# A seventh gate block ahead of the z blocks, 14 of its runs behind the last u, w products, and scan steps with 3 + 3 runs of projections

## The chip, the cores and the metric

The kernel runs on one core of a Trainium2 chip. The metric is the device time of one execution in microseconds; several executions are timed and their median is given. The engines are named as in the profile: PE (matrix products), PEld (its weight loads), DVE (vector), ACT (scalar and activation functions), POOL and SP (here used for issuing transfers). Each engine works through its own queue in order, and a transfer is issued by an engine's queue and lands some time later.

## The reference

One layer of a hybrid decoder block on x of 1 x 1024 x 1024, in float32. Two token mixers run on the same normalised input, each result is multiplied by its own SiLU gate path (z), projected up, weighted by per-channel sigmoid gates, summed and projected out; a residual add and a final RMSNorm follow. Mixer A is attention with three dilated windows. Mixer B, where the change acts, is a gated delta rule, computed in chunks of 64 tokens:

```python
def _gated_delta_rule(q, k, v, g, beta):
    ...
    t_inv = lax.linalg.triangular_solve(eye + a, jnp.broadcast_to(eye, a.shape),
                                        left_side=True, lower=True, unit_diagonal=True)
    u = t_inv @ (vc * bc[..., None])
    w = t_inv @ (k_beta * jnp.exp(G)[..., None])
    attn = jnp.einsum('bhnid,bhnjd->bhnij', qc, kc) * decay_incl
    ...
    def step(state, inp):
        q_e, at, u_c, w_c, k_d, dec = inp
        v_new = u_c - jnp.einsum('bhck,bhkv->bhcv', w_c, state)
        o = jnp.einsum('bhck,bhkv->bhcv', q_e, state) + jnp.einsum('bhij,bhjv->bhiv', at, v_new)
        state = state * dec[..., None, None] + jnp.einsum('bhck,bhcv->bhkv', k_d, v_new)
        return state, o
```

There are 8 heads and 16 chunks, so the scan has 16 steps, one after another.

## The kernel before

The large work of PE is the projections of the normalised input (h, held as a high and a low half in fp16) with the input weights (whi and wlo). The **feed** cuts these into units, one per block of 256 weight columns, and each unit into runs. A run is one `feed.tick(1)`: three products of 128x512 at L183, L184 and L185. Most units have 32 runs; some, among them gates 0, 6 and 7 and the four z blocks, are computed with seven products in place of eight (28 runs) and give their four outputs after runs 16, 20, 24 and 28. The feed takes the units in the order in which they were added. A unit's weights are loaded (L313, on POOL's queue) and split into halves (ACT at L330, DVE at L329 and L83) while the unit ahead of it still runs.

PE's order is written out by hand: everything on PE stands in program order. Wherever mixer B has to wait for another engine, the code calls `feed.tick(n)`, and n runs of projections stand between the two products that depend on each other. How many stand where is set by the constants at L44 to L72. The other engines are ordered by a scheduler by data and priorities.

The stages around the change, in program order:

- **Merge** (twice, for the head halves hb = 0 and 1): the triangular inverses are put together from 32x32 blocks (L1350, L1365). `MERGE_TICKS` runs stand in two gaps of each. Y is the intermediate result that DVE copies.
- **u, w products** (L1413, L1417), in two groups g for each hb. `UW_LAG[1][hb]` runs stand ahead of the first group and `UW_LAG[2]` behind each group but the last. Their results are copied to uw tiles (L1424, by DVE for u and by ACT for w) that share three buffers, and stored to un_d (POOL's queue, L1429) and wn_d (ACT's queue, L1426).
- **Pairs** (L1266): the score products of the chunks, in banks ps_S and ps_G. Right ahead of hb = 1's stand `Q_LAG[1]` = 4 runs. E, their masked result, is stored to a_d (POOL's queue, L1630). Sums and transposed products on ps_O (L1247) follow.
- `feed.until(("gate", 5))`, then the pools are changed; from there on gate outputs use a tile gst with two buffers in place of one.
- **Scan** (L1706, L1723, L1734): each step multiplies the state Sb with w and q (ps_S, L1706), DVE forms vn, PE multiplies vn with the decayed keys (ps_G, L1723), and DVE adds to Sb (L86 is the helper's line for these DVE operations). `PACE[0]` runs stand between L1706 and L1723, `PACE[1]` behind L1723. Each second step ends with the products of vn and the score matrix (L1734) into ob. `SCAN_LEAD` runs stand ahead of the first step.
- **Turn loops** (L1755): after `OB_LAG` runs, ob times the factor fac of its norm is transposed in four loops; two head pairs h0 by two halves hf. Each takes a bank of ps_G and one of ps_S, of which there are two each, and DVE multiplies them into zb, four writes a loop. Four runs stand behind each loop.

A gate output is a tanh of the product into gst (L948) and a store to gspa or gspb (L950); for two of a seven-product unit's four outputs DVE first combines product and rest into gst. A z output of mixer A (zs) is a SiLU, a product with mixer A's result (oa, loaded on SP's queue) and a split into osa; of mixer B a SiLU into zb. `UW_LAG` and the other constants are module constants; `state_side` calls the merge and the u, w products.

Of the kernel before, what the change touches and what calls it, by code (L numbers as in the profile page):

```python
# [51 lines left out]
K_LAG = 4  # L52
Q_LAG = (14, 4)
Q_SUMS = (8, 3)
PACE = (4, 3)
UW_LAG = (12, (10, 4), 6)
STATE_LAG = 12
OB_LAG = 12
ZS = 1
# [1 line left out]
OG = 2  # L61
TURN_LAG = 20
SUMS_AT = (4, 36, 68, 100)
MERGE_TICKS = 5
V_GAP = 8
GM_LAG = 2
BA_LAG = 8
# [10 lines left out]
def hybrid_block(ctx: ExitStack, tc: tile.TileContext, A):  # L78
# [13 lines left out]
    def bank(tag, bufs):  # L92
        return ps.tile([128, 512], F32, name=f"ps_{tag}", tag=tag, bufs=bufs)
# [99 lines left out]
    def proj(w, ct, hf, out):  # L193

        hi, lo = w
        p = bank("mm", 3)
        cs, ts = slice(ct * 128, ct * 128 + 128), slice(hf * 512, hf * 512 + 512)
        n = 0
        for _ in mm3_steps(p, (lambda k: hi[:, k, cs], lambda k: lo[:, k, cs]),
                           (lambda k: h_hi[:, k, ts], lambda k: h_lo[:, k, ts])):  # L200
            n += 1
            if n == KT:
                out(p)
            yield
# [150 lines left out]
    def seven_products(blocks, out, product=by_channel):  # L355

        x, q = bank("mm", 3), bank("mm", 3)

        def step(n, p, fn, first=False):
            for i, _ in enumerate(product(n, blocks[n], p, first)):  # L360
                if i == 3:
                    fn()
                yield

        def copy(dst, src):
            with tc.high_priority():
                SC.copy(dst, src)

        y, rest = [], []

        def seed_y():
            y.append(bank("mm", 3))
            copy(y[0], x)

        def keep():
            rest.append(wst.tile([128, 512], F32, name="x7", tag="x7", bufs=1))
            copy(rest[0], q)

        yield from step(0, x, seed_y, True)
        yield from step(1, q, keep, True)  # L380
        yield from step(2, x, lambda: copy(q, x))
        yield from step(3, y[0], lambda: out(0, 0, y[0], None))
        yield from step(4, q, lambda: out(1, 1, q, rest[0]))
        yield from step(5, x, lambda: out(1, 0, x, rest[0]))
        yield from step(6, q, lambda: out(0, 1, q, None))

    feed = Feed()

    def add_unit(name, unit, gen, gen7):
        if unit in SEVENS:  # L390
            feed.add(name, Seven(unit), gen7)
        else:
            feed.add(name, Normal(A["w"][unit]), gen)
# [526 lines left out]
    def gate_unit(i, out):  # L920
        br, u = ("a", i) if i < 4 else ("b", i - 4)

        def gen7(w):
            def take(c, hf, p, rest):
                with tc.high_priority():
                    out(br, 2 * u + c, hf, p, rest)

            yield from seven_products(w, take)

        def gen(w):  # L930
            for c in range(2):
                for hf in range(2):
                    def take(p):
                        with tc.high_priority():
                            out(br, 2 * u + c, hf, p)

                    yield from proj(w, c, hf, take)

        add_unit(("gate", i), U_GATE + i, gen, gen7)
# [399 lines left out]
    def merge(hb, T1p, bsp):  # L1339
# [4 lines left out]
        def left(g):  # L1344
            py = bank("S", 2)
            Y = p2_.tile([128, 16, 32], F32, name="Y", tag="rv", bufs=3)
            for n in range(16):
                for c2 in range(2):
                    r = 64 * c2
                    PE.matmul(py[r + 32:r + 64, n * 32:n * 32 + 32], lhsT=flat[r:r + 32, 16 * g + n, 32:64],  # L1350
                              rhs=T1p[r:r + 32, 4 * g + n // 4, n % 4], start=(n == 0), stop=True,
                              skip_group_check=True)
                    yield
            for c2 in range(2):
                r = slice(64 * c2 + 32, 64 * c2 + 64)
                with tc.high_priority():
                    TT(Y[r], py[r].rearrange("p (n i) -> p n i", i=32), bc(bsp[r, 16 * g:16 * g + 16], 32), ALU.mult)
            Ys[g] = Y

        def right(g):  # L1360
            pu, Y = bank("G", 2), Ys[g]
            for n in range(16):
                for c2 in range(2):
                    r = 64 * c2
                    PE.matmul(pu[r:r + 32, n * 32:n * 32 + 32], lhsT=Y[r + 32:r + 64, n],  # L1365
                              rhs=flat[r + 32:r + 64, 16 * g + n, 32:64], start=(n == 0), stop=True,
                              skip_group_check=True)
                    yield
            for c2 in range(2):
                r = slice(64 * c2, 64 * c2 + 32)  # L1370
                with tc.high_priority():
                    SC.copy(flat[r, 16 * g:16 * g + 16, 32:64], pu[r].rearrange("p (n i) -> p n i", i=32))

        Ys = {}
        for _ in left(0):
            pass
        feed.tick(MERGE_TICKS)
        for _ in zip_longest(left(1), right(0)):
            pass
        feed.tick(MERGE_TICKS)  # L1380
        for _ in right(1):
            pass

    def state_parts(hb):

        def load(g):
            ts = slice(4 * g, 4 * g + 4)
            rv = p2_.tile([128, 4, 4, 64], F32, name="rvt", tag="vT", bufs=2)

            tag = ("As", "X")[g] if hb else "vT"  # L1390
            kb = p2_.tile([128, 4, 4, 64], F32, name="kbt", tag=tag, bufs=1 if hb else 2)
            nc.sync.dma_start(out=rv, in_=rv_d[ts, :, 4 * hb:4 * hb + 4].rearrange("t p h v -> p t h v"))
            nc.sync.dma_start(out=kb, in_=kb_d[hb][:, ts])
            return rv, kb
# [3 lines left out]
        for g in range(2):  # L1398
            if g and not hb:
                loads.append(load(g))  # L1400
                feed.tick(UW_LAG[0])
            rv, kb = loads[g]
# [53 lines left out]
    for hb in range(2):  # L1456
        conv_unit(hb, 0, lambda c, hb=hb: qT[2 * hb + c],
                  lambda c, q, hb=hb: nc.scalar.dma_start(out=q_d[2 * hb + c], in_=q))
    gate_unit(5, gate_spill)
    side, solved, packs = [], [], []  # L1460
    for hb in range(2):
        decay(hb)
# [11 lines left out]
    def z_unit(br, u, take):  # L1474
        def gen(w):
            def out(c, hf, p, rest):
                with tc.high_priority():
                    take(br, 2 * u + c, hf, p, rest)

            yield from seven_products(w, out)  # L1480

        feed.add(("z", br, u), Seven(U_Z + 2 * (br == "b") + u), gen)
# [26 lines left out]
        z_unit("a", u, z_now)  # L1509
    for u in range(2):  # L1510
        z_unit("b", u, z_keep)
    for i in (6, 7):
        gate_unit(i, gate_spill)

# [116 lines left out]
    def state_side(hb):  # L1633
        parts = state_parts(hb)
        next(parts)
        merge(hb, solved[hb], packs[hb])
        feed.tick(UW_LAG[1][hb])
        for g, _ in enumerate(parts):
            if not (hb and g):
                feed.tick(UW_LAG[2])  # L1640

    state_side(0)
    for hb in range(2):
# [5 lines left out]
        if hb == 0:  # L1649
            feed.tick(STATE_LAG)  # L1650
            state_side(1)
    feed.until(("gate", 5))
    feed.flush()
    pctx.close()
    fp = ctx.enter_context(tc.tile_pool(name="fin", bufs=1))
# [17 lines left out]
    for t in range(8):  # L1673
# [21 lines left out]
        for c2 in range(2):  # L1695
# [19 lines left out]
            else:  # L1715
                GP.memset(ov, 0.0)
                feed.tick(SCAN_LEAD)
            feed.tick(PACE[0])
            pS = [bank("G", 2), bank("G", 2)]
# [5 lines left out]
            with tc.high_priority():  # L1725
                for hb in range(2):
                    sv = Sb[:, 2 * hb:2 * hb + 2]
                    TT(sv, sv, hv(pS[hb][:, :128]), ALU.add)
            feed.tick(PACE[1])
        po = bank("G", 2)  # L1730
# [18 lines left out]
    for h0 in (0, 2):  # L1749
        for hf in range(2):  # L1750
            ts = slice(hf * 512, hf * 512 + 512)
            ps2 = [bank("G", 2), bank("S", 2)]
            for t in range(4):
                for c2 in range(2):
                    PE.transpose(ps2[c2][:, 128 * t:128 * t + 128],  # L1755
                                 ob[:, 4 * hf + t, 4 * c2 + h0:4 * c2 + h0 + 2].rearrange("p h v -> p (h v)"), ident)
            for hb in range(2):
                ct = 2 * hb + h0 // 2
                zv = zs[ct][:, ts].rearrange("p (t c i) -> p t c i", c=2, i=64)
                for c2 in range(2):  # L1760
                    zc = zv[:, :, c2]
                    STT(zc, ps2[c2].rearrange("p (t b i) -> p t b i", b=2, i=64)[:, :, c2 ^ hb], gnw, zc,
                        ALU.mult, ALU.mult)
                if ("b", ct) not in osp:
                    osp["b", ct] = fpb.tile([128, 2, S], F16, name=f"osb{ct}", tag="oTb", bufs=6)
                n = osp["b", ct]
                sc = H_SCALE
                SC.activation(n[:, 0, ts], zs[ct][:, ts], AF.Copy, scale=sc)
                STT(n[:, 1, ts], zs[ct][:, ts], sc, n[:, 0, ts], ALU.mult, ALU.subtract)
            feed.tick(4)  # L1770
    feed.until(("gate", 6))
    feed.tick(1)
    cctx.close()
    gs_.close()
# [272 lines left out]
```

## Time and profile before

| | us |
|---|---|
| median of 3 executions | 1074.67 |
| lowest, highest | 1073.64, 1075.37 |
| profiled execution, its own time | 1076.42 |
| its span in the trace | 1074.6 |
| mean granted clock of PE | 0.997 of full |

The stretch that the change touches, by the profiled execution (us from the span's start):

| stage | PE from |
|---|---|
| hb = 1's last u, w products end | 757.9 |
| hb = 1's first pairs (L1266) | 760.6 |
| scan, first step with a state | 789.5 |
| run behind the scan's last products | 883.5 |
| first and fourth turn loop | 891.3, 902.4 |

How rows are read: a row of the order of time is start, duration, engine, line, operation, output <- inputs, shapes and count, and in brackets how long the engine stood idle just before and what ended that. A row of the waits is what waited, for what, total us, times and the longest. A row of windows is the stretch, its length, the busy time (and number of instructions) of PE, PEld, DVE, ACT and POOL, PE's granted clock, the transfers' share and their GB/s; with a tile named it holds only the busy time on that tile. PE's matmuls overlap, so a duration of 0.38 stands beside a start every 0.22.

### The profile page before, as it was taken

The page shows a single profiled execution, that of the slowest core. Times are in us where ns is not written, and L with a number is a line of the kernel's source. Part 1 is how long each engine was busy: PE and PEld are TensorE (multiplying, and loading weights), DVE is VectorE, ACT ScalarE, POOL GpSimd, SP SyncE. Part 2 cuts the span into 40 slices and gives each one's busy share as a digit, 9 for nine tenths or more (in the row PEclk, how much of TensorE's full clock was granted, in tenths as well). Part 3 has the DMA queues.
Part 4 walks back from the last instruction along what each step waited for, and adds up shares of the span by engine and source line. Part 5 has one row for each costly group of instructions (what it writes and reads, how often), then busy time and mean ns, then how long its engine had stood idle before and what let it go on. Part 6 is the DMA issues. An engine that isn't in the chain of part 4 may idle for free.

```text
span 1074.6 us, 23700 instructions
## 1 busy us (share of the span) xinstructions
PE 1048.8 (98%) x9410; PEld 640.7 (60%) x9410; DVE 864.8 (80%) x1986; ACT 560.9 (52%) x1274; POOL 56.3 (5%) x107
## 2 busy tenths in 40 slices
PE   7999999999999999999999999999999999999997
PEld 5994685775956855765645545555555555444444
DVE  6997997869879779979966997986488679899844
ACT  6455766566666656547735733234344346343523
POOL 0000000000000000000000000110200000000000
PEclk9999999999999999999999999999999999999999
DMA  8144531632625432641234357786685433763132
GB/s 278 60 133 103 139 104 54 171 98 87 181 69 154 108 103 63 177 115 46 76 123 165 84 130 205 237 240 164 184 267 174 140 99 116 286 209 123 48 131 79
DMA packets 99776, 148.47 MB, mean 138 GB/s; under 512 B 31168, under 2 KB 64704, under 8 KB 98512
## 3 DMA queue, kind: packets, MB, share of 16 engines
q1 hardware_dynamic: 69264, 84.64, 27.3%
q0 software_dynamic: 12320, 44.11, 13.1%
q10 hardware_dynamic: 18080, 18.20, 4.9%
q8 instruction: 74, 1.21, 0.5%
q14 instruction: 38, 0.31, 0.1%
HBM read 91.13 MB, written 36.90 MB: 119 GB/s over the span
## 4 chain that ended last, share of the span: by engine, by line
PE 60%; DVE 27%; ACT 5%; issue 3%; DMA 3%; SPq 1%; ACTq 0%; DVEq 0%
PE ps_mm L183 14%; PE ps_mm L184 14%; PE ps_mm L185 14%; DVE ca L83 4%; DVE wlo L83 2%; DVE X L86 2%; DVE stmp L86 2%; DVE sm L799 2%; PE ps_S L185 2%; PE ps_S L184 2%; PE ps_S L183 2%; DVE tl L86 1%; PE ps_G L813 1%; DVE rt L86 1%; ACT sm L803 1%
## 5 line engine op out<-in xcount | busy, mean ns | idle before, releaser
L185 PE MATMUL ps_mm<-h_hi,wlo 128*128 128x512 f16 (+1 forms) x552 | 207.9, 377 | 0.0
L183 PE MATMUL ps_mm<-h_hi,whi 128*128 128x512 f16 (+1 forms) x492 | 185.5, 377 | 0.0
L184 PE MATMUL ps_mm<-h_lo,whi 128*128 128x512 f16 (+1 forms) x492 | 185.3, 377 | 0.0
L185 PEld LDWEIGHTS <-wlo 128*128 128x128 f16 x788 | 77.2, 98 | 86.5 <-issue 0.7
L183 PEld LDWEIGHTS <-whi 128*128 128x128 f16 x848 | 83.3, 98 | 69.1 <-issue 0.6
L184 PEld LDWEIGHTS <-whi 128*128 128x128 f16 x848 | 83.1, 98 | 67.9 <-issue 0.9
L183 PE MATMUL ps_mm<-whi,h_hi 128*128 128x256 f16 x384 | 105.1, 274 | 0.0
L185 PE MATMUL ps_mm<-whi,h_lo 128*128 128x256 f16 x384 | 104.7, 273 | 0.0
L184 PE MATMUL ps_mm<-wlo,h_hi 128*128 128x256 f16 x384 | 104.7, 273 | 0.0
L803 ACT ACTIVATE sm<-sm,osb 128x128 f32<-128x128 f32 (+1 forms) x160 | 69.5, 435 | 65.3 <-DVE osb L799 58.7
L86 DVE TENSOR_TENSOR tl<-ps_G,th 128x256 f16<-128x256 f32 (+1 forms) x96 | 51.8, 539 | 22.1 <-ACT th L818 21.6
L799 DVE CUSTOM_DVE_ANT_0 sm<-ps_S,amask 128x128 f32<-128x128 f32 (+1 forms) x192 | 59.2, 345 | 6.0 <-PE ps_S L792 5.9
L83 DVE SCALAR_TENSOR_TENSOR wlo<-wstage,whi 128x1024 f16<-128x1024 f32 x50 | 60.9, 1217 | 3.4 <-ACT whi L166 3.2
L83 DVE SCALAR_TENSOR_TENSOR ca<-xc,cw,ca 128x512 f32<-128x512 f32 x72 | 53.8, 747 | 5.5 <-ACT ca L1010 4.8
L166 ACT ACTIVATE whi<-wstage 128x1024 f16<-128x1024 f32 x49 | 51.4, 1051 | 1.7 <-ACT gst L948 0.8
L813 PE MATMUL ps_G<-cons,sm 128*128 128x128 f32 x280 | 47.9, 275 | 3.2 <-ACT sm L803 1.5
L83 DVE SCALAR_TENSOR_TENSOR whi<-wstage,whi 128x512 f16<-128x512 f32 x60 | 40.8, 687 | 12.3 <-ACT whi L330 11.7
L330 ACT ACTIVATE whi<-wstage 128x512 f16<-128x512 f32 x60 | 37.1, 626 | 19.6 <-DVE wstage L329 13.3
L813 PEld LDWEIGHTS ps_G<-cons,sm 128*128 128x128 f32 x280 | 35.5, 141 | 19.4 <-ACT sm L803 5.0
L184 PEld LDWEIGHTS <-h_hi 128*128 128x128 f16 x384 | 45.8, 119 | 1.6
L183 PE MATMUL ps_mm<-h_hi,wlo 128*128 128x512 f16 x120 | 45.6, 380 | 1.0 <-DVE rx L83 1.0
L183 PEld LDWEIGHTS <-h_hi 128*128 128x128 f16 x384 | 45.5, 119 | 1.5
(459 smaller groups left out, 2595.7 us busy)
## 6 DMA issues: line engine op xcount, KB each, us to landing
wstage<-in_w POOLq DMA_DIRECT2D x68, 512.0 KB, 4.5
og<-osb ACTq DMA_DIRECT2D x32, 132.0 KB, 2.2
og<-og SPq DMA_DIRECT2D x32, 132.0 KB, 2.2
gspb<-gst ACTq DMA_DIRECT2D x16, 256.0 KB, 2.4
sga<-gspa SPq DMA_DIRECT2D x8, 512.0 KB, 6.5
wstage<-in_w_up POOLq DMA_DIRECT2D x8, 512.0 KB, 4.7
wos<-in_w_out SPq DMA_DIRECT2D x8, 512.0 KB, 5.3
sgb<-gspb SPq DMA_DIRECT2D x8, 512.0 KB, 4.9
```

What stands on the lines that cost most here:

```text
L83: (eng or V).scalar_tensor_tensor(out, in0, scalar, in1, op0=op0, op1=op1)
L86: (eng or V).tensor_tensor(out, in0, in1, op)
L166: in_turn(SC.activation(hi[:, 4 * c:4 * c + 4], st, AF.Copy, scale=W_SCALE))
L183: PE.matmul(out, lhsT=wh(k), rhs=mh(k), start=first and i == 0, stop=False, skip_group_check=True)
L184: PE.matmul(out, lhsT=wh(k), rhs=ml(k), start=False, stop=False, skip_group_check=True)
L185: last_pe[0] = PE.matmul(out, lhsT=wl(k), rhs=mh(k), start=False, stop=last and i == len(ks) - 1, skip_group_check=True).ins.name
L330: in_turn(SC.activation(t[:, b, 0], self.part[name], AF.Copy, scale=W_SCALE))
L799: V.tensor_tensor_reduce(P[:, u, :128 * nk], psc[:, u * 256:u * 256 + 128 * nk], mask, -cexp, -NEG, ALU.add, ALU.min, accum_out=osb[:, 256 ...
L803: SC.activation(P[:, u, :128 * nk], P[:, u, :128 * nk], AF.Exp, bias=osb[:, 256 + hd:257 + hd], scale=-1.0, accum_out=osb[:, 260 + hd:261 ...
L813: PE.transpose(pt[:, c:c + 128], P[:, u, i * 128:i * 128 + 128], ident)
```

## The change

Gate 6 is put into the feed right behind gate 5, ahead of the z blocks; gate 7 stays behind them. The number of runs in all stays the same, and their places between the other products change: 3 runs in place of 4 between L1706 and L1723 of each scan step (16 fewer), 2 in place of 4 behind each turn loop (8 fewer), 14 behind the last u, w products of hb = 1 where none were (with the 4 that follow, 18), 6 in place of 4 ahead of hb = 1's first, and 6 in place of 5 in the two gaps of each merge. The feed is run to the end of gate 6, not 5, ahead of the scan, so gate 6 uses the earlier pool's single gst buffer; the later `feed.until(("gate", 6))` is left out. Lines behind L1459 of the old kernel move by one or two (L1706, L1723, L1755 become L1705, L1722, L1754).

```diff
-PACE = (4, 3)
-UW_LAG = (12, (10, 4), 6)
+PACE = (3, 3)
+UW_LAG = (12, (10, 6), 6, 14)
...
-MERGE_TICKS = 5
+MERGE_TICKS = 6
...
-    gate_unit(5, gate_spill)
+    for i in (5, 6):
+        gate_unit(i, gate_spill)
...
-    for i in (6, 7):
-        gate_unit(i, gate_spill)
+    gate_unit(7, gate_spill)
...
         for g, _ in enumerate(parts):
-            if not (hb and g):
-                feed.tick(UW_LAG[2])
+            feed.tick(UW_LAG[2 + (hb and g)])
...
-    feed.until(("gate", 5))
+    feed.until(("gate", 6))
     feed.flush()
...
-            feed.tick(4)
-    feed.until(("gate", 6))
+            feed.tick(2)
     feed.tick(1)
```

Three places show how the other engines' queues follow. The first is ACT's queue around the four copies of hb = 1's w products (uw<-ps_S), before:

```order
L1424 COPY uw<-ps_S 128x512
L1426 DMA wn_d<-uw 128x4x128
L330 ACTIVATE whi<-wstage 128x512
L1424 COPY uw<-ps_S 128x512
L1426 DMA wn_d<-uw 128x4x128
L330 ACTIVATE whi<-wstage 128x512
L1424 COPY uw<-ps_S 128x512
L1426 DMA wn_d<-uw 128x4x128
L948 ACTIVATE gst<-ps_mm 128x512
L950 DMA gspb_10376<-gst 128x512
L1424 COPY uw<-ps_S 128x512
L1426 DMA wn_d<-uw 128x4x128
```

and after:

```order
L1424 COPY uw<-ps_S 128x512
L1426 DMA wn_d<-uw 128x4x128
L948 ACTIVATE gst<-ps_mm 128x512
L950 DMA gspb_10294<-gst 128x512
L1424 COPY uw<-ps_S 128x512
L1426 DMA wn_d<-uw 128x4x128
L330 ACTIVATE wlo<-wstage 128x512
L1424 COPY uw<-ps_S 128x512
L1426 DMA wn_d<-uw 128x4x128
L330 ACTIVATE wlo<-wstage 128x512
L330 ACTIVATE whi<-wstage 128x512
L1424 COPY uw<-ps_S 128x512
```

The gate outputs and weight splits that stand between the copies are others, but the four copies keep their order and no more than two other operations come between two of them.

The second is DVE's queue in the scan, between the update of the state by its decay (Sb<-Sb,dec) of one early step and vn of the next, before:

```order
L86 TENSOR_TENSOR ob<-ps_S,eGs 128x2x64 x2
L86 TENSOR_TENSOR Sb<-Sb,dec 128x256
L86 TENSOR_TENSOR Sb<-Sb,ps_G 128x128 x2
L86 TENSOR_TENSOR vn<-un,ps_S 128x128 x2
L86 TENSOR_TENSOR ob<-ps_S,eGs 128x2x64 x2
```

and after:

```order
L86 TENSOR_TENSOR ob<-ps_S,eGs 128x2x64
L86 TENSOR_TENSOR Sb<-Sb,dec 128x256
L83 SCALAR_TENSOR_TENSOR wlo<-wstage,wlo 128x512
L86 TENSOR_TENSOR Sb<-Sb,ps_G 128x128
L83 SCALAR_TENSOR_TENSOR zs<-ps_mm,x_10719 128x512
L86 TENSOR_TENSOR Sb<-Sb,ps_G 128x128
L329 TENSOR_TENSOR wstage<-wstage 128x512
L83 SCALAR_TENSOR_TENSOR zs<-zs,oa 128x512
L83 SCALAR_TENSOR_TENSOR whi<-wstage,whi 128x512
L86 TENSOR_TENSOR vn<-un,ps_S 128x128 x2
```

A z block's output stands between the two halves of the state's sum now, and four operations of splits and z outputs stand in this step that stood elsewhere.

The third is DVE's queue from the scan's last sum (ob<-ob,ps_G) to the eight products of ob with fac that the turn loops need, before:

```order
L86 TENSOR_TENSOR ob<-ob,ps_G 128x512
L329 TENSOR_TENSOR wstage<-wstage 128x512
L83 SCALAR_TENSOR_TENSOR gst<-ps_mm,x_11860 128x512
L1740 TENSOR_REDUCE oss<-sq 128x8
L83 SCALAR_TENSOR_TENSOR wlo<-wstage,wlo 128x512
L83 SCALAR_TENSOR_TENSOR fac<-oss,rqs 128x64
L83 SCALAR_TENSOR_TENSOR wlo<-wstage,wlo 128x512
L83 SCALAR_TENSOR_TENSOR gst<-ps_mm,x_11860 128x512
L329 TENSOR_TENSOR wstage<-wstage 128x512
L1745 RECIPROCAL fac<-fac 128x64
L86 TENSOR_TENSOR ob<-ob,fac 128x512 x8
```

and after:

```order
L86 TENSOR_TENSOR ob<-ob,ps_G 128x512
L83 SCALAR_TENSOR_TENSOR wlo<-wstage,wlo 128x512
L1739 TENSOR_REDUCE oss<-sq 128x8
L83 SCALAR_TENSOR_TENSOR fac<-oss,rqs 128x64
L83 SCALAR_TENSOR_TENSOR zb_11962<-ps_mm,x_11812 128x512
L329 TENSOR_TENSOR wstage<-wstage 128x512
L1744 RECIPROCAL fac<-fac 128x64
L86 TENSOR_TENSOR ob<-ob,fac 128x512 x8
```

Three operations that stood behind the last sum (a sum of two weight blocks in wstage, a split wlo and a block's output) stand ahead of it now, and the output that is left behind it is one of z block b1 in place of gate 6.

## The prediction

> **What bounds the kernel now.** I read the page's busy times and its chain first, then the waits of PE by engine, then PE's own order of time around each wait, and last the engine that PE waited for there.
>
> ```profile
> PE 1048.8 (98%) x9410; PEld 640.7 (60%) x9410; DVE 864.8 (80%) x1986; ACT 560.9 (52%) x1274; POOL 56.3 (5%) x107
> PE 60%; DVE 27%; ACT 5%; issue 3%; DMA 3%; SPq 1%; ACTq 0%; DVEq 0%
> ...
> PE ps_S L1266 <- ACT uw L1424: 2.3, 1, 2.3
> ...
> PE ps_S L1755 <- DVE zb L83: 0.5, 1, 0.5
> PE ps_O L1247 <- DVE rq L1251: 0.4, 1, 0.4
> PE ps_G L1365 <- DVE Y L86: 0.4, 1, 0.4
> ...
> PE ps_S L1417 <- DMA kbt<-kb_d: 0.3, 1, 0.3
> 785.00:884.00 99.00, 99.00 (x1330) 51.19 (x1328) 76.32 (x191) 41.53 (x72) 4.24 (x8) 1.00 0.55 172
> ```
>
> PE is busy for 98% of the span, and the change leaves its matmuls the same in number and kind. So the time can move only by what PE waits, and by its clock. The five waits shown are those in the stretch that the change touches; the longer ones in the list lie earlier, in stages it leaves alone. The last row is the scan (stretch, length, busy time of PE, PEld, DVE, ACT and POOL, then PE's clock): PE fills all 99.00 us and DVE is busy for 76.32, or 77%. There is no wait to win inside the scan; shorter steps there only take cover away. The prize is the first wait:
>
> ```profile
> 757.90 0.39 PE L183 MATMUL ps_mm<-h_hi,whi 128*128 128x512 f16 x1
> ...
> 760.59 0.33 PE L1266 MATMUL ps_S<-qT,kT 64*64 64x64 f32 x2
> 763.22 1.55 PE L1266 MATMUL ps_S<-qT,kT 64*64 64x64 f32 x62 [2.30 <-ACT uw L1424]
> 764.70 0.61 PE L183 MATMUL ps_mm<-h_hi,whi 128*128 128x512 f16 x1
> ...
> 767.22 0.38 PE L183 MATMUL ps_mm<-h_hi,whi 128*128 128x512 f16 x1
> ...
> 758.55 0.59 ACT L1424 COPY uw<-ps_S 128x512 f32<-128x512 f32 x1 [1.52 <-DMA wn_d<-uw]
> 762.58 0.59 ACT L1424 COPY uw<-ps_S 128x512 f32<-128x512 f32 x1 [2.35 <-DMA wn_d<-uw]
> 760.60:764.80 4.20, 1.90 (x66) 1.64 (x66) 0.00 (x0) 1.22 (x2) 0.79 (x2) 0.88 0.89 220
> 764.80:768.50 3.70, 3.70 (x12) 1.28 (x11) 3.18 (x5) 0.63 (x1) 0.56 (x1) 0.68 0.51 185
> ```
>
> The last u, w product has ended when the run at 757.90 starts. Four runs follow (757.90 to 760.50, so 0.65 us a run), then the score products of L1266 want the bank that the fourth uw copy empties. That copy starts only at 762.58, since its uw buffer (three of them) waits for a store to land, and ends at 763.17. From the last product to the free bank: 5.3 us; cover: 2.6 us. The clock then falls: 0.88 and 0.68 in the two windows, together (0.12 x 4.20 + 0.32 x 3.70) x 2 = 3.4 us at half speed, in which two runs take 764.70 to 767.22, 2.52 us in place of 1.30.
>
> **The change part by part.**
>
> *A. 18 runs in place of 4 behind the last u, w products.* 18 x 0.65 = 11.7 us of cover against 5.3. Nothing else is late there, even if the copy slipped by 6 us. Gone are the wait (760.59 to 763.22 less two products, 2.5 us) and the half clock (1.2 us on the two runs, 0.4 on the products between): **-4.1**.
>
> *B. Two more runs around hb = 1's merge and two more ahead of its first u, w products.* The Y wait is 0.39 with one more run (0.65) in front of it: gone, with its restart some 0.5. The kbt wait of 0.3 belongs to hb = 0, which gets one run more in each merge gap too, but the DMA's issue moves along with the merge; I take 0.1. Bounds 0 and 0.9: **-0.6**.
>
> *C. Gate 6 ahead of the z blocks.* Its 28 runs, one load of weights with three splits, four tanh and four stores move from the end of the scan to the stretch from the u, w products to the scan's lead. The loads now stand on POOL's queue between the un_d stores and hb = 1's a_d stores, whose first reader comes some 25 runs later; this costs nothing. On SP, z a0's first two oa loads fall behind the loads of the scan's first chunk instead of ahead of them, and are read 28 runs later than before: nothing. The tanh and the store's issue now stand between the uw copies on ACT, under A's cover of 6 us. But gate 6 now writes to a pool with one gst buffer where it had two:
>
> ```profile
> 749.78 0.60 ACT L948 ACTIVATE gst<-ps_mm 128x512 f32<-128x512 f32 x1
> 750.41 0.33 ACTq L950 DMA_DIRECT2D gspb<-gst  x1
> ...
> 885.04 0.69 DVE L83 SCALAR_TENSOR_TENSOR gst<-ps_mm,x 128x512 f32<-128x512 f32 x1
> ...
> gspb<-gst ACTq DMA_DIRECT2D x16, 256.0 KB, 2.4
> ```
>
> One output is 0.6 + 0.3 + 2.4 = 3.3 us from tanh to landing, and two of the four have a DVE combination of 0.69 before. Outputs come every four runs, 2.6 us, with other matmuls between, up to 3.7. The fourth tanh holds a bank that z a0's second product wants four runs later. Below, nothing (cover reaches); above, 2 us (all four landings late). An output every 3.7 against 3.3 to 4.0 is near the first: **+0.4**.
>
> *D. Scan steps with 3 + 3 runs.* Between the products with the state (L1706) and those that need vn (L1723) PE has 4 runs, soon 3.
>
> ```profile
> 789.81 0.41 PE L1706 MATMUL ps_S<-Sb,qt 64*64 64x64 f32 x16
> ...
> 792.85 0.46 PE L1723 MATMUL ps_G<-vn,kdec 64*64 64x64 f32 x16
> ...
> 824.45 0.46 PE L1723 MATMUL ps_G<-vn,kdec 64*64 64x64 f32 x16
> ...
> 792.00 0.47 DVE L86 TENSOR_TENSOR vn<-un,ps_S 128x128 f32<-128x128 f32 x2
> ...
> 823.88 0.47 DVE L86 TENSOR_TENSOR vn<-un,ps_S 128x128 f32<-128x128 f32 x2
> ...
> 827.66 0.48 DVE L86 TENSOR_TENSOR vn<-un,ps_S 128x128 f32<-128x128 f32 x2 [0.78 <-PE ps_S L1706]
> ...
> 785.00:884.00 99.00, 7.20 (x30) 1.00 0.55 172
> 785.00:884.00 99.00, 13.85 (x47) 1.00 0.55 172
> 785.00:884.00 99.00, 12.39 (x38) 1.00 0.55 172
> ```
>
> In the step at 790, vn ends at 792.47, 0.38 before PE wants it; with one run fewer it would be late by 0.27. DVE was not slow but busy: z block a1 stands in its queue. Four of the 15 steps are like this (the first at 792.00, the last at 823.88, which ends at 824.35, 0.10 before 824.45), late by 0.27, 0.52, 0.33 and 0.55 with the old order: 1.7 us. In the others DVE waits for PE, as at 827.66, and vn has some 2 us to spare. The order of DVE's queue is another after the change; following it, row by row with these durations, one state update is split by a z operation and the delays come to about 0.6. Bounds 0 and 2.5 (six steps at 0.42, the mean of the four): **+0.6**. DVE's load rises little: without its own 39 us (the last three rows, DVE's work on vn, Sb and ob, and eight sums of 0.68) the scan holds 37.4 us for 110 runs; with 93 runs it is 31.6, and 70.5 of 88.6 us are 80%, from 77%.
>
> *E. Two runs in place of four in each turn loop.* The loops use two pairs of banks, so the third waits until zb of the first has been written.
>
> ```profile
> 883.54 0.39 PE L183 MATMUL ps_mm<-sum4h,whi 128*128 128x512 f16 x1
> ...
> 891.32 0.27 PE L1755 MATMUL ps_G<-cons,ob 128*128 128x128 f32 x1
> ...
> 898.30 0.27 PE L1755 MATMUL ps_G<-cons,ob 128*128 128x128 f32 x1
> 899.05 0.30 PE L1755 MATMUL ps_S<-cons,ob 128*128 128x128 f32 x1 [0.48 <-DVE zb L83]
> ...
> 889.42 4.91 DVE L86 TENSOR_TENSOR ob<-ob,fac 128x512 f32<-128x512 f32 x8
> ...
> 896.05 0.48 DVE L83 SCALAR_TENSOR_TENSOR zb<-ps_G,cons,zb 128x256 f32<-128x256 f32 x1
> ...
> 897.44 0.48 DVE L83 SCALAR_TENSOR_TENSOR zb<-ps_G,cons,zb 128x256 f32<-128x256 f32 x1
> ...
> 898.43 0.47 DVE L83 SCALAR_TENSOR_TENSOR zb<-ps_S,cons,zb 128x256 f32<-128x256 f32 x1
> ...
> 890.00:895.00 5.00, 5.00 (x29) 2.84 (x28) 5.00 (x10) 2.66 (x5) 0.00 (x0) 1.00 0.29 107
> ```
>
> Take 883.54, where the run behind the scan's last product starts, as zero. The first loop is wanted at +7.8 (12 runs), before and after. The third is wanted at +14.8 now and is held until +15.5; with four runs fewer (2.6) it is wanted at +12.2. DVE has no idle time here (5.00 of 5.00 us): the eight products with fac end at +10.8, the zb writes start at +12.5, and of the first loop's four the third ends 1.8 and the last 2.8 later; these two free the banks. In DVE's new order two splits and one block output of 0.6 each that stood behind the scan's last sum stand ahead of it, since the scan ends two runs later in the feed. But the output still behind it waits for its product, four runs after zero, so I count only 1.1 of these 1.8 us and start zb at +11.4: one bank is free at +13.2, the other at +14.2, and PE waits 1.0 + 1.0. The fourth loop, then wanted at +16.4, waits for the second's last zb, at about +17.1: 0.7. The sum is 2.7, less the 0.6 that was: **+2.1**. Bounds: zb two us earlier, 0; zb as late as now, +3.2.
>
> A wait of 2.0 us asks for the clock. The trace before has 1.35 us without work that kept it (the window below: 3.65 of 5.00 us busy, clock 1.00), and the 2.30 at 763 that lost it. 2.0 in two pieces lies between, nearer to the second by its length, but it is broken by a product; I count no loss and make it a rival.
>
> ```profile
> 461.00:466.00 5.00, 3.65 (x46) 3.21 (x43) 3.55 (x9) 0.74 (x2) 0.00 (x0) 1.00 0.50 118
> ```
>
> [...] By the trace, E is 2.1 or, with the clock lost, 3.8.
>
> *F.* Changes between runs and other matmuls cost some 0.1 each way: **+0.1**. What stands behind the loops (gate 7, up, out) keeps its runs; gate 7's last tanh moves behind splits of the output weights on ACT, and its bank is wanted about 4 us later than I put that tanh: nothing.
>
> *Sum:* -4.1 - 0.6 + 0.4 + 0.6 + 2.1 + 0.1 = -1.5 us. The profiled execution took 1076.42 us around its span of 1074.6; the median of the runs is 1074.67, lower by 1.75. Set against the median: **1073.2 us**, -0.14%. A measurement of this kernel can tell about 0.2% (2.15 us) from no change.
>
> **The rivals.**
>
> *R1, the loops cost little.* If the zb writes start 1.5 us earlier than I put them, because more of DVE's splits and gate work fall ahead of the scan's end, E is +0.6, and D nothing: -4.1 - 0.6 + 0.4 + 0.6 + 0.1 = -3.6, 1071.1 us. For it: gate 6's DVE work has left this place. Against it: z b1 puts its own there, and DVE was never idle here.
>
> *R2, slower: the scan becomes bound by DVE.* Place: the wait for vn at L1723 in each step. Price: 0.42 us a step, the mean of the four late steps. In the trace they fall where a z block's outputs lie in DVE's queue; after, z blocks run through 93 runs with fewer others. If 12 of the 15 steps are so, D is 5.0 in place of 0.6: +2.9, 1077.6 us. It decides from D = 2.1, five late steps, where the change breaks even; from ten it is slower by over 0.2%. Against it: 80% load, and the easy steps have 2 us to spare.
>
> *R3, the clock falls in the third loop.* 1.7 us more (half of 3.4): +0.2, 1074.9 us, no change. For it: the 2.30 at 763. Against it: two pieces.
>
> *R4, the wait only moves:* if gate 6's tanh delayed the fourth uw copy by over 6 us, A would shrink. ACT has 0.6 us pieces and nothing of that length; I give it no more than R3's tail.
>
> **How the numbers follow.** Forecast 0.45, R1 0.33, R2 0.10, R3 with R4 0.12. The forecast's own range is 1072 to 1075. The whole range goes from all costs at nothing (-4.7, 1070.0) to 1076.5, which leaves out most of R2 and a little of R1. Faster by over 0.2% (below 1072.5): R1 and 0.06 of the forecast, 0.39. Slower by over 0.2% (above 1076.8): R2 and 0.02 of R3, 0.12. Within: the rest, 0.49.
>
> **What would show it.** A: no wait for uw at L1266, and a clock of 1.00 there. B: no wait for Y. C: waits of PE for gst, or of a run for a bank, around z a0's first runs. D: waits of L1722 (the new number) for vn, in few steps, 0.2 to 0.6 each. E: two waits for zb in the third loop and one in the fourth, 2.7 together; a window with the clock below 1.00 there means R3. What would make it wrong most likely is E's start of zb, which I followed by hand, and a queue that delays z a0's weights, so that runs wait for whi.

## The result and the profile after

The changed kernel takes 1078.14 us (median of 6 executions, 1077.39 to 1080.60) against 1074.03 us of the kernel before (median of 6). The ratio is 1.0039, 95% interval 1.0026 to 1.0052: slower by 4.1 us, between 2.8 and 5.6, where 1.5 us less was forecast. The profiled execution of the change took 1077.39 us around a span of 1075.6. First its busy times and PE's waits (what waited, for what, us in total, times, longest) in the stretch that was changed:

```profile
PE 1047.5 (97%) x9410; PEld 639.7 (59%) x9410; DVE 864.1 (80%) x1986; ACT 561.3 (52%) x1274; POOL 57.1 (5%) x107
...
PE ps_G L1722 <- DMA qt<-q_d: 2.0, 1, 2.0
PE ps_S L1705 <- DVE Sb L86: 1.3, 2, 0.7
...
PE ps_S L1754 <- DVE zb L83: 1.2, 2, 0.7
...
PE ps_G L1754 <- DVE zb L83: 0.9, 1, 0.9
...
PE ps_G L1733 <- DVE Sb L86: 0.5, 1, 0.5
PE ps_O L1247 <- DVE rq L1251: 0.3, 1, 0.3
```

The waits for uw, Y and kbt are gone (the one for kbt was also missing when the kernel before was profiled a second time, below). In their place stand one of 2.0 for the loads of the scan's first step, three for the state Sb, and three for zb. The windows of 25 us (columns as before: length, busy PE, PEld, DVE, ACT, POOL, then PE's clock) show where PE lost time:

```profile
750.00:775.00 25.00, 25.00 (x457) 13.86 (x459) 11.81 (x19) 9.96 (x18) 6.72 (x11) 1.00 0.56 160
775.00:800.00 25.00, 22.95 (x196) 11.61 (x189) 15.08 (x33) 10.72 (x19) 1.92 (x4) 1.00 0.60 207
800.00:825.00 25.00, 24.30 (x339) 12.71 (x337) 21.42 (x55) 10.91 (x18) 1.06 (x2) 1.00 0.82 265
825.00:850.00 25.00, 23.76 (x353) 12.69 (x352) 20.51 (x52) 11.10 (x19) 1.06 (x2) 1.00 0.47 144
...
875.00:900.00 25.00, 23.36 (x203) 12.55 (x202) 22.07 (x47) 13.40 (x21) 1.06 (x2) 1.00 0.10 34
```

The stretch with the old wait (750 to 775) is full, at full clock. The scan, which had no wait, now has idle time in its first, second and third window, and the turn loops (875 to 900) have more than the 0.48 us they had. Taking the excess of every interval between two matmuls over its usual length, the change lost 2.0 us in the scan's first step, 2.6 in the other steps (0.2 to 0.8 in a few, and some smaller ones) and 2.6 in the turn loops, where 0.7 was before. It won 2.3 at the uw wait, 0.6 at Y and 0.3 at the u, w products, by the second profile of the kernel before that is shown below. Together that is a loss of 3.3 (and 0.2 at rq), and the two spans, 1071.9 and 1075.6, differ by 3.7. The first profile, whose span of 1074.6 is only 1.0 less, had lost the clock besides.

### The profile page after: what moved, and what is told of

Its sections match the earlier page's. It is cut to its first block, busy times and chain, and to the rows that moved or that the text cites. A ratio compares the mean times of both kernels' runs of the same rounds, so it can differ in the third digit from the quotient of the medians.

```text
span 1075.6 us, 23712 instructions
## 1 busy us (share of the span) xinstructions
PE 1047.5 (97%) x9410; PEld 639.7 (59%) x9410; DVE 864.1 (80%) x1986; ACT 561.3 (52%) x1274; POOL 57.1 (5%) x107
## 4 chain that ended last, share of the span: by engine, by line
PE 75%; DVE 16%; ACT 3%; DMA 2%; issue 2%; SPq 2%; DVEq 0%; ACTq 0%
PE ps_mm L183 18%; PE ps_mm L185 18%; PE ps_mm L184 18%; PE ps_G L813 2%; DVE ca L83 2%; PE ps_S L185 2%; PE ps_S L183 2%; PE ps_S L184 2%; DVE wlo L83 1%; SPq L629 1%; DVE sm L799 1%; DVE tl L86 1%; DVE rt L86 1%; PE ps_G L185 1%; PE ps_G L184 1%
## 5 line engine op out<-in xcount | busy, mean ns | idle before, releaser
L185 PEld LDWEIGHTS <-h_lo 128*128 128x128 f16 x384 | 45.5, 119 | 1.4
```

The lines of the kernel that those rows point to most:

```text
L185: last_pe[0] = PE.matmul(out, lhsT=wl(k), rhs=mh(k), start=False, stop=last and i == len(ks) - 1, skip_group_check=True).ins.name
```

## The experiments

### Was the first profile typical? The kernel before again

No edit; one more profiled execution.

> The kernel before, profiled once more. Theory T1 (the wait for uw and the half clock behind it are there in every execution, so the change removed 4.1 us each time): the wait for uw at L1266 is again 2.0 to 2.6 us, the clock falls behind it, and the span is near 1074.6. Rival T2 (the first profile was one of the executions in which the wait was long; mostly it is shorter and the clock holds, so the change removed less): the wait is under 1.5 us, no window between 755 and 770 has a clock below 1.00, and the span is near 1072.2 (the median of 1074.03 less the 1.8 that lies around the span).

Its span was 1071.9 us, 2.7 less than the first, with a time of 1073.66. PE's order at the uw wait, and the window around it:

```profile
759.64 0.33 PE L1266 MATMUL ps_S<-qT,kT 64*64 64x64 f32 x2
762.08 1.14 PE L1266 MATMUL ps_S<-qT,kT 64*64 64x64 f32 x60 [2.11 <-ACT uw L1424]
...
750.00:775.00 25.00, 22.79 (x380) 12.94 (x373) 13.54 (x21) 9.93 (x17) 7.22 (x12) 1.00 0.62 189
```

The wait is there again, 2.11 after 2.30, but the clock held: 1.00 where the first profile had 0.93 over the same 25 us. So neither theory held as it was put. The wait is in both executions, the half clock behind it in one of them. Of the 46 timed executions of the kernel before that were taken beside these experiments, on two chips, 15 had a mean clock of 0.997 or lower and 31 of 0.998 or 0.999; on each chip the median of the former stood 1.6 to 1.8 us above that of the latter, and half of 3.4 us at half speed is 1.7. The first profile, 1076.42, was one of the former third.

### The uw wait by itself

```diff
-            ps2 = [bank(n, 2) for n in ("GG", "SS")[(t0 // 4) ^ (src is not kT)]]
+            ps2 = [bank(n, 2) for n in ("GG", "SS")[(t0 // 4) ^ (src is not kT and hb == 0)]]
```

This is the kernel before, in which hb = 1's score products take the ps_G banks first, which DVE empties early (by 759.2 in the first trace of the kernel before, where ACT emptied the last ps_S bank at 763.2), and ps_S four runs later. No run moves.

> The kernel before with one condition changed: the second pairs of hb = 1 begin with the ps_G banks and take ps_S after the four runs, so that the late uw copy has some 4 us more; no run moves. It measures part A by itself. If the wait for uw costs its length (2.1 us in the second profile of before, 2.3 and a half clock in the first), the ratio is 0.9980, and 0.9965 if most executions also lose the clock. If the wait only moves on (to the ps_S products four runs later, or to the scan), it is 0.999 to 1.000.

1071.83 us (1071.47 to 1072.45), ratio 0.9973 (0.9962 to 0.9984). PE's order there, and ACT's last uw copy:

```profile
760.86 1.16 PE L1266 MATMUL ps_G<-qT,kT 64*64 64x64 f32 x64
764.65 1.16 PE L1266 MATMUL ps_S<-qT,kT 64*64 64x64 f32 x64
...
761.82 0.58 ACT L1424 COPY uw<-ps_S 128x512 f32<-128x512 f32 x1 [1.53 <-DMA wn_d<-uw]
```

The copy is as late as ever (it ends at 762.40), but what needs its bank now comes at 764.65, and PE waits for neither. The gain is 2.9 us (1.7 to 4.1): the wait of 2.1 to 2.3, and the clock's loss as often as it came. None of its 7 executions had a clock below 0.998. This version beats both kernels, and it is part A by itself: worth 2.9 us, with the forecast's 4.1 at the very end of the interval.

### The turn loops

```diff
-            feed.tick(2)
+            feed.tick(4)
```

> The changed kernel with four runs behind each turn loop again. If the waits for zb in the third and fourth loop (1.11 + 0.88 + 0.64 in the trace of the change, 0.64 before) cost their length, 2.0 us go: ratio to before 1.0020 in place of 1.0039, and one wait of some 0.6 stays in the third loop. If the time only moves to the next wait, the ratio stays near 1.0039.

1075.36 us, ratio 1.0007 (0.9998 to 1.0016), with no wait for zb, where one of some 0.6 was expected to stay. The fall from 1.0039 is 3.4 us, more than the 2.6 of all three waits, but the intervals leave room: the difference of the two ratios is uncertain by some 1.7 us. The waits for Sb (1.2) are still there, and so are waits for the scan's loads, 2.7 in all here (1.0 for kdec, 1.3 for wt, 0.4 for qt). In the change's own trace the loops came as forecast, in DVE's and PE's order:

```profile
888.44 4.90 DVE L86 TENSOR_TENSOR ob<-ob,fac 128x512 f32<-128x512 f32 x8
...
895.07 0.47 DVE L83 SCALAR_TENSOR_TENSOR zb<-ps_G,cons,zb 128x256 f32<-128x256 f32 x1
...
897.45 0.48 DVE L83 SCALAR_TENSOR_TENSOR zb<-ps_S,cons,zb 128x256 f32<-128x256 f32 x1
...
897.08 0.30 PE L1754 MATMUL ps_G<-cons,ob 128*128 128x128 f32 x1 [0.95 <-DVE zb L83]
898.07 0.30 PE L1754 MATMUL ps_S<-cons,ob 128*128 128x128 f32 x1 [0.69 <-DVE zb L83]
900.91 0.30 PE L1754 MATMUL ps_S<-cons,ob 128*128 128x128 f32 x1 [0.48 <-DVE zb L83]
```

Zero here is 883.85, where the run behind the scan's last products starts: zb starts at +11.2 (forecast +11.4), and the two banks of the third loop come free so that it starts at +13.2 and +14.2 (forecast the same).

### The scan's first step

```diff
-SCAN_LEAD = 6
+SCAN_LEAD = 10
```

> The changed kernel with four more runs (2.6 us) ahead of the scan's first step (SCAN_LEAD 10). If that step waits for its loads (2.0 us in the trace of the change, none before), the wait goes and the ratio falls by 0.0019 to about 1.0020. If the loads are late by more in most executions than in the profiled one, it falls by more, up to 0.0024, the length of the four runs. If it only moves to later steps, the ratio stays at 1.0039.

1073.95 us, ratio 1.0004 (0.9994 to 1.0015): 3.7 us better than the change, where 2.0 to 2.6 was expected. The first step's wait is gone, and the loops lose 1.1 in place of 2.6, since the scan ends four runs later in the feed and other splits stand between ob and zb. In this kernel zb starts right behind the products with fac, with no split between the first four writes:

```profile
890.67 4.89 DVE L86 TENSOR_TENSOR ob<-ob,fac 128x512 f32<-128x512 f32 x8
895.48 0.47 DVE L83 SCALAR_TENSOR_TENSOR zb<-ps_G,cons,zb 128x256 f32<-128x256 f32 x1
...
896.66 0.47 DVE L83 SCALAR_TENSOR_TENSOR zb<-ps_S,cons,zb 128x256 f32<-128x256 f32 x1
```

1.2 us from the first to the fourth write, where the change had 2.4. So this run tells the first step's wait (2.0) together with over half of the loops' (1.5), not alone. Of the scan's waits for Sb, 1.8 in the change, 1.2 stayed. Two of its 12 executions took 1077.21 and 1079.09 us at a mean clock of 0.997; the trace is of another one, so what they waited for is open.

Why the first step waits is seen in POOL's and SP's order of the change, and in the time its transfers took to land (name, queue, count, KB, median us):

```profile
785.86 0.54 POOL L313 DMA_DIRECT2D wstage<-in_w  x1 [7.64 <-DVE wstage L329]
...
787.39 0.54 POOL L313 DMA_DIRECT2D wstage<-in_w  x1 [0.41 <-DVE wlo L83]
...
786.68 0.34 SPq L1685 DMA_DIRECT2D vn<-un_d  x1
787.07 0.42 SPq L1686 DMA_DIRECT2D kdec<-kd_d  x1
...
788.68 0.37 SPq L1689 DMA_DIRECT2D un<-un_d  x1
...
vn<-un_d SPq DMA_DIRECT2D x1, 128.0 KB, 3.6
kdec<-kd_d SPq DMA_DIRECT2D x1, 256.0 KB, 6.9
qt<-q_d SPq DMA_DIRECT2D x1, 256.0 KB, 8.0
...
794.44 0.46 PE L1722 MATMUL ps_G<-vn,kdec 64*64 64x64 f32 x16 [1.97 <-DMA qt<-q_d]
```

The weights of z block a1, two pieces of 512 KB, are issued within 2 us of the first step's five loads. The row of L1722 names qt, but that product reads vn and kdec alone, and qt, issued at 788.02, landed at 796.0, when PE had gone on. vn landed at 790.3, early enough; kdec, issued at 787.07, landed at 794.0, right ahead of 794.44. So the late load is kdec. In the kernel before the same loads were issued with no weights beside them, and landed sooner:

```profile
vn<-un_d SPq DMA_DIRECT2D x1, 128.0 KB, 2.1
kdec<-kd_d SPq DMA_DIRECT2D x1, 256.0 KB, 3.3
```

To tell this from a lead that is merely short, z a1's weights were held back behind the first state update (their load also loses its high priority with the scheduler):

```diff
-                for at, fn in zip(src.AFTER_SEVEN if busy else src.AFTER, steps):
+                ats = (12, 20, 23, 26) if self.units[i][0] == ("z", "a", 1) else src.AFTER_SEVEN if busy else src.AFTER
+                for at, fn in zip(ats, steps):
...
-            with tc.high_priority():
+            with ExitStack() if self.late else tc.high_priority():
...
+                    if self.late:
+                        in_turn(V.memset(st[:, 0, :1], 0.0))
                     nc.gpsimd.dma_start(out=st, in_=self.src[n])
```

> The changed kernel, but the weights of z block a1 are loaded only after the scan's first state update (a one-column memset that DVE does there stands ahead of the load, and the splits come later: 20, 23, 26 runs instead of 14, 20, 26). Theory: the first step waits because two pieces of 512 KB are issued within 1 us of its five loads and both share the DMA engines. Then the first loads land in 3 to 5 us as in the kernel before, the wait of 2.0 us falls below 0.5, and the ratio falls from 1.0039 to about 1.002 unless the later splits cost something. Rival: the first step is late because its loads are issued only 5.7 us ahead; then they land in 7 to 8 us again and the wait stays.

```profile
kdec<-kd_d SPq DMA_DIRECT2D x1, 256.0 KB, 3.0
...
793.53 0.46 PE L1725 MATMUL ps_G<-vn,kdec 64*64 64x64 f32 x16
...
804.23 0.46 PE L1708 MATMUL ps_S<-Sb,wt 64*64 64x64 f32 x16 [2.00 <-DMA wt<-wn_d]
```

kdec lands in 3.0 us and the first step (L1725 here) no longer waits, although kdec is again issued only 5.3 us ahead of it (788.19, against 5.4 us ahead of the time at which PE began to wait in the change): the weights beside the loads were the cause. But the time got worse, 1081.88 us, ratio 1.0061 (1.0048 to 1.0075): the weights, now issued at 795.11, meet the next loads of the scan, whose wt (issued at 795.43) lands in 8.7 us and is 2.0 late in turn, and the clock fell there (0.93 from 800 to 825). In the kernel before, the weights in the scan were issued at 797.75 and 799.30 and no load of kdec, wt, qt or un within 3 us of them.

### The scan's steps

```diff
-            feed.tick(PACE[0])
+            feed.tick(PACE[0] + (0 < ch < 12))
```

> The changed kernel with 4 + 3 runs again in the scan steps 1 to 11, 3 + 3 in the last four. If the waits for Sb (0.20 + 0.77 + 0.58 + 0.80 in the trace of the change) come from the run that was taken out of each step, 2.4 us go: ratio about 1.0017. If they come from the z blocks' place in the scan and DVE's new order, they stay, and the ratio is 1.003 to 1.004.

1074.00 us, ratio 0.9996 (0.9987 to 1.0004). Of the waits for Sb 0.2 us was left:

```profile
PE ps_G L1722 <- DMA wt<-wn_d: 1.8, 1, 1.8
...
PE ps_mm L185 <- DVE wlo L83: 0.7, 1, 0.7
...
PE ps_S L1705 <- DVE Sb L86: 0.2, 1, 0.2
```

So the scan's waits come from the run that was taken out. The added runs move the z blocks' outputs among the steps as well, but so did the longer lead, and there 1.2 of the 1.8 stayed. The loops' waits are gone here too, as with the longer lead, and a new wait of 0.7 for wlo stands behind them: with 11 runs more ahead of it the output weights are split a little late. The first step's wait stays (1.8, in the first row). The forecast of 1.0017 took the 2.4 us alone.

How a state update came late is seen in DVE's order of the change in the step from 803 on (the place shown with the change), and in PE's:

```profile
804.38 0.47 DVE L86 TENSOR_TENSOR vn<-un,ps_S 128x128 f32<-128x128 f32 x2
...
806.97 0.41 DVE L86 TENSOR_TENSOR Sb<-Sb,dec 128x256 f32<-128x256 f32 x1
807.31 0.68 DVE L83 SCALAR_TENSOR_TENSOR wlo<-wstage,wlo 128x512 f16<-128x512 f32 x1
807.91 0.27 DVE L86 TENSOR_TENSOR Sb<-Sb,ps_G 128x128 f32<-128x128 f32 x1
808.11 0.68 DVE L83 SCALAR_TENSOR_TENSOR zs<-ps_mm,x 128x512 f32<-128x512 f32 x1
808.71 0.27 DVE L86 TENSOR_TENSOR Sb<-Sb,ps_G 128x128 f32<-128x128 f32 x1
...
809.12 0.40 PE L1705 MATMUL ps_S<-Sb,wt 64*64 64x64 f32 x11 [0.56 <-DVE Sb L86]
```

vn is written at 804.38, in time. It is the sum into Sb that ends at 808.98, and the next products with the state, begun at 808.24, wait for its second half.

### The remaining two

Lead and pace together:

```diff
-SCAN_LEAD = 6
+SCAN_LEAD = 10
...
-            feed.tick(PACE[0])
+            feed.tick(PACE[0] + (0 < ch < 8))
```

> The changed kernel with four more runs ahead of the first step and 4 + 3 runs in steps 1 to 7. If the three costs found (first step's loads 2.0, Sb in the scan 2.4, turn loops 2.0) are independent, and the loops' waits go wherever the scan ends 4 to 11 runs later in the feed, as with lead10 and pace4x11, the excess falls by another 1 to 1.6 us below lead10's: ratio 0.9985. If the 11 runs are too many for what stands behind (a wait for wlo of 0.85 at the output weights in pace4x11), it is 0.9995.

1073.13 us, ratio 0.9982 (0.9973 to 0.9991). The placement of gate 6 is thus worth something once the scan has its runs back, but less than the one condition of the second experiment: this trace has a wait of 0.7 for wlo at the output weights and one of 1.8 for rq ahead of the scan.

The changed kernel once more:

> The changed kernel, profiled once more. The median of its times, 1078.14, would be a span of 1076.35; the profiled one was 1075.6. The waits of the turn loops (2.6) and of the scan (2.4) come out the same; the wait for the first step's loads differs between executions and is 2 to 3.5 us here.

1079.86 us around a span of 1078.1. The waits are those of the first trace, 2.0 for the first step's loads among them, not longer. The window behind that wait says what differs:

```profile
775.00:800.00 25.00, 22.90 (x194) 11.31 (x185) 13.71 (x28) 10.44 (x19) 1.91 (x4) 0.93 0.59 207
...
795.00:799.00 4.00, 4.00 (x29) 1.35 (x25) 1.74 (x4) 1.11 (x2) 0.00 (x0) 0.57 0.75 249
```

Here the clock fell (0.57 over 4 us, again 3.4 us at half speed), behind a wait that in the first trace of the same kernel had cost no clock. The two spans differ by 2.5 us, of which the clock accounts for 1.7.

## Why the prediction was wrong, by its own steps

- **The first reading and its base.** Correct was that only waits and clock could move the time, and that the prize was the uw wait. Wrong was to take one profiled execution as the kernel: its half clock (1.6 us) was booked in full as a gain in A, and the sum was then set against a median of executions of which only a third had it.
- **A, -4.1: mis-sized.** The wait went and nothing else was late there (750 to 775 full). By itself it is worth 2.9 us (1.7 to 4.1): the wait was 2.1 to 2.3 where 2.5 was booked, and the half clock is there in a third of the executions.
- **B, -0.6:** Y went, and so did the wait within the u, w products: 0.6 + 0.3, at the upper bound.
- **C, +0.4: the outputs right, the load missed.** The single gst buffer cost PE nothing that shows, and rq's second wait some 0.2. But C moved a unit boundary: z a1's weights are now issued beside the first step's loads. The part named POOL's and SP's queues and looked at the order in them only, not at what is in flight at once; it put this at nothing. It cost 2.0 us in both traces, since kdec landed in 6.9 us in place of 3.3, and the clock in one of them. Of the terms that the forecast had too small this and D are the largest.
- **D, +0.6: mis-sized, and in the wrong place.** 2.6 us, just above the upper bound of 2.5. The part checked vn ahead of L1723 and not Sb ahead of L1706. vn came in time, as at 804.38; the sum into Sb came behind splits and z outputs, and the waits are for it, or for the banks that it reads (L1733). R2 named the right engine and the wrong operand; its price (0.42 a step) would have fitted six steps.
- **E, +2.1: right**, 1.9, both its times and its two pieces. The clock held in both traces (1.00 from 875 to 900) at the two pieces, 0.95 and 0.69 in the first, so R3 did not come about at the loops. A loss of the length that it priced came at the first step, in the second trace.
- **R1 fell:** zb started 0.2 earlier than I put it, not 1.5.
- **The sum with what was measured:** -2.9 - 0.9 + 0.2 + 2.0 + 2.6 + 1.9 = +2.9. The clock behind the first step adds some 0.2 by an estimate: of the seven executions of the change, six timed and one profiled, only the last had a mean clock of 0.997 or lower, and 1.7 / 7 = 0.2. That gives +3.1, within the measured 2.8 to 5.6 but 1.0 below the 4.1; where that 1.0 lies is open, and F was not measured by itself.

## What to carry to other kernels

A wait can often be removed where it is: taking the bank that is free first won 2.9 us, while moving runs of cover to the same place took them from the scan's steps and the turn loops, which had lived on them. When a unit of work is moved, look up what its loads will be in flight with (kdec landed in 6.9 us beside the weights, in 3.0 and 3.3 without them), not only what they are queued behind. And before a half clock or any one-off of a few us is booked as a gain, look at a second execution: the clocks listed with the timed runs were enough to tell.

## What the runs showed of the hardware

A wait of PE of about 2 us cost the clock in some executions and not in others, with the same kernel: 2.30 lost it and 2.11 kept it in the kernel before, and in the change the first step's wait of 1.97 kept it in one trace, while the next trace, with a wait of the same 2.0, lost it. The two losses whose windows are shown (0.50 over 3.41 us below, 0.57 over 4.00 us above) were each 3.4 us at half speed, about 1.7 us of time. Two waits of 0.95 and 0.69 with a product between kept it (1.00 from 875 to 900). The kernel with four runs behind each loop has no wait of 2 us for its loads, but 1.0 (kdec), 1.3 (wt) and 0.4 (qt); the mean clock of its trace is 0.997, where the change's first trace has 0.999.

Rows of 3.41 us at such waits (length, busy PE, PEld, DVE, ACT, POOL, then the clock) are, for the kernel before (two windows), its second profile, the change and the kernel with four runs behind each loop:

```profile
760.36:763.77 3.41, 1.11 (x40) 0.74 (x42) 0.00 (x0) 0.75 (x2) 1.03 (x2) 1.00 0.97 208
763.77:767.18 3.41, 3.41 (x48) 1.70 (x38) 2.37 (x4) 0.92 (x2) 0.56 (x1) 0.50 0.51 157
...
760.38:763.80 3.42, 1.73 (x65) 1.33 (x66) 0.53 (x1) 1.22 (x2) 0.06 (x1) 1.00 0.84 213
...
790.80:794.21 3.41, 1.67 (x8) 0.59 (x6) 0.00 (x0) 0.35 (x1) 0.00 (x0) 1.00 0.96 346
...
802.11:805.52 3.41, 1.69 (x38) 1.05 (x37) 1.82 (x6) 1.49 (x3) 0.00 (x0) 1.00 1.08 350
```

The 1.11 us of PE's work in the first row stand right ahead of the half clock. With 1.73 in the third row and 1.67 in the fourth the clock held (1.00 from 750 to 775 and from 775 to 800). The 1.69 of the last row stand in the trace with the mean clock of 0.997; since the ends of products are modelled, 1.67 and 1.69 can't be told apart. The 2.30 lay whole in the first row's stretch, and 1.70 of the 2.11 in the third row's. What decides whether a wait of some 2 us costs the clock was not shown: no edit moved such a wait in time and left its length as it was.

The first step's loads of 128 and 256 KB landed in 2.1 us (vn) and 3.3 us (kdec) with no weights beside them, and in 3.6 and 6.9 when 1 MB of weights was issued within 2 us of them. With the weights held back kdec landed in 3.0.
